# A gated attention block on one core: products of ones before x, weight loads in pieces, closer last merges, more buffers in the tail

## The chip, the cores and the metric

The kernel runs on one core of a Trainium2 chip. A core has TensorE (PE, matrix products into PSUM; its weight loads are shown as PEld), VectorE (DVE), ScalarE (ACT) and GpSimd (POOL) for elementwise work, and SyncE (SP), which here issues every DMA, in order, on one queue. The metric is the device time of one execution in microseconds, given as the median of several runs. The kernel before took 2000.66 us (three runs, 1995.67 to 2001.24).

## The reference

One encoder layer over x of 2048 x 1024 float32. h is the RMS norm of x. One projection of h gives the queries, keys and values of two attention mixers, two gate paths and two merge gates:

```
qa, ka, va, qb, kb, vb, ga, gb, mg = split(h @ w_in)
ya = banded_attention(norm(qa), norm(ka), va, window 128, sink) * silu(ga)      # 8 heads, 2 key heads
yb = sum_g alpha_g * dilated_group(norm(qb_g), norm(kb_g), vb_g) * silu(gb)     # g: dilation 1, 4, 16; 8 heads each
merged = sigmoid(mg_0 + b_0) * (ya @ w_branch_a) + sigmoid(mg_1 + b_1) * (yb @ w_branch_b)
out = x + merged @ w_out
```

alpha is a softmax over the three groups' log-denominators, so the three groups of one pair of heads must be merged before their gate is applied.

## The kernel before

**Precision.** Every product is made of float16 pairs: an operand v is scaled by a power of two and split into a high part (a copy on ACT) and a low part (v minus high, on DVE); three products, high x high, high x low, low x high, are summed in PSUM. So each operand, the weights too, passes ACT and DVE before TensorE can use it. The scale of a weight tile comes from the sum of its squares: a gain on POOL, squares on ACT, a product with a matrix of ones on TensorE that adds over the partitions (`norm_sum`), and a few small steps on DVE (`norm_pow`).

**Order.** The program's order on each engine is written out by hand. A heap of planned times holds small steps; `at(t, f)` adds one, and `until(t)` emits all that are due. While products are emitted, `until` is called between them, so that the steps fall at planned places of TensorE's stream. The planned times only set the order in each engine's queue; on the chip each instruction waits for its operands. `chain` adds steps that must follow one another and try again 0.04 later where a PSUM bank is held.

**Start.** The time is in microseconds. x comes in 16 tiles (`x_load`), each is squared (ACT), scaled (DVE), transposed by TensorE in two halves (`x_turn`) and split into XH and XL. The first two gate chunks (`g_step`) are multiplied in between, from the time when tiles 0 to 3 are there.

**Main part.** The time is in slots. There are 14 units (2 of mixer A, 12 of mixer B: four pairs of heads by three groups) of 8 slots each, so NPAIR = 112. In a slot, TensorE makes the 48 projection products of two 128-row subsets; some slots hold one more product of a gate chunk (FILLS, 24 products). From a subset come norm steps and a DMA transpose of keys and queries (`turn`, tile kq); some 2.9 slots later, an item takes logits, maxima (DVE), exponentials (ACT), the split, a DMA transpose (tile pt) and, LV slots behind its start, the products with the values (`values`, tile pv). Groups 1 and 2 are stored to DRAM (zd) and loaded again (zz) where group 0 merges (`b_merge_q`), whose sums (ya) are turned by TensorE into the one PSUM bank pt, gated and stored to DRAM (`YPart`, tile ytd). The weights of the next unit (`w_load`), of gate chunks (`g_load`) and pieces of w_branch and w_out (`piece_load`, of which only squares are taken) pass one after the other through one raw buffer, wraw. Their loads stand in SP's queue among the transposes.

**Drain.** After slot 112 there are no more projections; slots 112 to 116 and 118 hold 48 fill products each, beside the last items and merges.

**Tail.** Again in microseconds. First five times eight merge-gate products (`gate_pair`, `job(5.2, ...)`), while w_out and the next weights are prepared (`prep`, `b_load`, `b_blocks`). Then 32 branch steps (`branch_pair`, 24 products each): gates come from DRAM (`gate_load`, tiles kp and fg), y in four quarters of eight chunks (`y_part`, tile yg, split into Y), branch weights through `br_load`; sums of them (`a_blocks`) are split into mm and stored to DRAM (mtd). At last 56 products of 12 (`group`) of those blocks (`m_load`, tile M) with w_out's, in a fast scheme with seven products for eight, added to x and stored.

## Time and profile before

| | |
|---|---|
| runs (us) | 1995.67, 2000.66, 2001.24 |
| profiled execution: time, span (us) | 1997.88, 1996.1 |
| granted TensorE clock, mean | 0.998 |
| busy PE, DVE, ACT, POOL (us) | 1941.3, 1308.6, 1032.5, 944.1 |
| products | 17570 |
| DMA | 308.45 MB, mean 155 GB/s |

A line of a profile names engine, source line and operation, the tile written and the tiles read, and counts. The chain of waits is the work that ended last, followed back. A row of a wait names who waited for whom. A stretch's row gives, behind the two ends and the length, each engine's busy time (PE, PEld, DVE, ACT, POOL, each with the number of instructions), the granted share of TensorE's clock, the DMA engines' share and GB/s. SPq is SP's queue of DMA issues.

### The profile page before, as it was taken

The page shows a single profiled execution, that of the slowest core. Times are in us where ns is not written, and L with a number is a line of the kernel's source. Part 1 is how long each engine was busy: PE and PEld are TensorE (multiplying, and loading weights), DVE is VectorE, ACT ScalarE, POOL GpSimd, SP SyncE. Part 2 cuts the span into 40 slices and gives each one's busy share as a digit, 9 for nine tenths or more (in the row PEclk, how much of TensorE's full clock was granted, in tenths as well). Part 3 has the DMA queues.
Part 4 walks back from the last instruction along what each step waited for, and adds up shares of the span by engine and source line. Part 5 has one row for each costly group of instructions (what it writes and reads, how often), then busy time and mean ns, then how long its engine had stood idle before and what let it go on. Part 6 is the DMA issues. An engine that isn't in the chain of part 4 may idle for free. (4 is left out here: it accounts for less than half of the span.)

```text
span 1996.1 us, 47810 instructions
## 1 busy us (share of the span) xinstructions
PE 1941.3 (97%) x17570; PEld 1388.7 (70%) x17570; DVE 1308.6 (66%) x3484; ACT 1032.5 (52%) x2369; POOL 944.1 (47%) x2431
## 2 busy tenths in 40 slices
PE   5999999999999999999999899999999999999999
PEld 3567896678878898888989889897544444444444
DVE  6678877887768876677776887768542323765522
ACT  6467655776555566555666555655433433432200
POOL 3254556454547665556666666656311000222533
PEclk9999999999999999999999999999999999999999
DMA  6249986897749696486866877567523325778763
GB/s 245 79 85 172 177 159 138 145 191 146 178 89 198 117 174 148 99 186 131 173 123 129 160 151 152 100 122 142 153 92 116 132 86 183 207 207 260 253 235 145
DMA packets 584316, 308.45 MB, mean 155 GB/s; under 512 B 457488, under 2 KB 526224, under 8 KB 581776
## 3 DMA queue, kind: packets, MB, share of 16 engines
q1 hardware_dynamic: 584080, 305.39, 65.2%
q8 instruction: 137, 2.24, 0.5%
q14 instruction: 99, 0.81, 0.1%
HBM read 129.91 MB, written 65.27 MB: 98 GB/s over the span
## 5 line engine op out<-in xcount | busy, mean ns | idle before, releaser
L627 PE MATMUL pj<-wl,XH 128*128 128x128 f16 (+2 forms) x2816 | 714.2, 268 | 0.0
L627 PE MATMUL pj<-wh,XL 128*128 128x128 f16 (+2 forms) x2816 | 711.6, 269 | 0.0
L627 PE MATMUL pj<-wh,XH 128*128 128x128 f16 (+2 forms) x2816 | 708.0, 268 | 1.3 <-DVE vt L663 1.3
L627 PEld LDWEIGHTS <-XH 128*128 128x128 f16 x5632 | 577.6, 113 | 64.0 <-issue 1.8
L627 PEld LDWEIGHTS <-XL 128*128 128x128 f16 x2816 | 317.0, 113 | 26.1
L792 DVE CUSTOM_DVE_ANT_0 pr<-s,b,ubuf 128x256 f32<-128x256 f32 (+3 forms) x512 | 218.9, 464 | 57.7 <-PE s L777 55.6
L298 PEld LDWEIGHTS <-wh 128*128 128x128 f16 x1280 | 125.6, 98 | 158.6 <-issue 8.3
L259 POOL TENSOR_TENSOR rs_t<-rs_y 128x8 f32<-128x8 f32 (+2 forms) x345 | 112.2, 325 | 210.4 <-DVE rs_y L250 161.1
L809 DVE SCALAR_TENSOR_TENSOR p<-pr,p 128x512 f16<-128x512 f32 (+2 forms) x256 | 185.2, 723 | 7.8 <-ACT p L805 7.1
L694 POOL TENSOR_TENSOR rw<-rw,g 128x128 f32<-128x128 f32 (+1 forms) x224 | 139.5, 643 | 80.3 <-DVE rw L687 64.0
L687 DVE TENSOR_TENSOR rw<-rw,qr 128x512 f32<-128x512 f32 (+1 forms) x112 | 115.4, 1030 | 90.9 <-POOL vt L656 58.4
L169 POOL TENSOR_TENSOR wraw<-wraw,gn 128x768 f32<-128x768 f32 (+1 forms) x80 | 108.2, 1359 | 122.2 <-DMA wraw<-in_w_mrg_dram 122.2
L805 ACT ACTIVATE p<-pr 128x512 f16<-128x512 f32 (+2 forms) x256 | 159.2, 622 | 10.3 <-DMA pt<-p 4.0
L298 PE MATMUL fps<-Y,wh 128*128 128x512 f16 x512 | 153.8, 381 | 8.6 <-DVE fg L1349 2.0
L645 ACT ACTIVATE rw<-pj 128x256 f32<-128x256 f32 (+1 forms) x224 | 86.5, 386 | 140.4 <-PE pj L627 139.3
L777 PE MATMUL s<-kq 128*128 128x128 f16 (+1 forms) x1856 | 147.1, 218 | 5.6 <-DMA kq<-spl 5.6
L777 PEld LDWEIGHTS <-kq 128*128 128x128 f16 x2016 | 129.9, 98 | 29.0 <-issue 5.7
L709 POOL COPY spl<-spl 128x256 f16<-128x256 f16 (+1 forms) x224 | 92.4, 442 | 121.9 <-DVE spl L704 115.6
L1356 POOL TENSOR_TENSOR kp<-kp,fg 128x512 f32<-128x512 f32 x32 | 43.7, 1366 | 223.8 <-DVE fg L1349 216.6
L1409 PE MATMUL fps<-wt,M 128*128 128x512 f16 x672 | 145.5, 379 | 1.1 <-DVE pr L1423 0.9
L298 PE MATMUL pj<-XH,gh 128*128 128x512 f16 x384 | 145.8, 380 | 0.0
L298 PE MATMUL pj<-XL,gh 128*128 128x512 f16 x384 | 145.7, 380 | 0.0
(190 smaller groups left out, 3632.0 us busy)
## 6 DMA issues: line engine op xcount, KB each, us to landing
wraw<-in_w_units_dram SPq DMA_DIRECT2D x56, 384.0 KB, 4.5
mtd<-mm SPq DMA_DIRECT2D x56, 256.0 KB, 3.0
M<-mtd SPq DMA_DIRECT2D x8, 1792.0 KB, 9.6
mgd<-fg SPq DMA_DIRECT2D x40, 256.0 KB, 2.1
zd<-z SPq DMA_DIRECT2D x128, 66.0 KB, 2.0
zz<-zd SPq DMA_DIRECT2D x64, 132.0 KB, 2.9
xt<-in_x_dram SPq DMA_DIRECT2D x16, 512.0 KB, 10.2
gtd<-yo SPq DMA_DIRECT2D x32, 256.0 KB, 2.8
```

The costliest lines, as they stand in the source:

```text
L169: G.tensor_tensor(v, v, gn[:, c0:c0 + 2].unsqueeze(2).to_broadcast([128, 2, n]), OP.mult)
L259: G.tensor_tensor(tv, yv, yv, OP.mult)
L298: out.append(lambda w=w, xx=xx, ch=ch, i=i: T.matmul(ps[:], lhsT=w[:, ch, c0:c0 + 128], rhs=xx[:, ch, ts], start=(i == 0), stop=(i == n - 1)))
L627: out.append(lambda lhs=lhs, rhs=rhs, ch=ch, a=a, b=b, k=k: T.matmul(ps[:, a:b], lhsT=lhs[:, ch, :], rhs=rhs[:, ch, a:b], start=(k == 0), ...
L687: V.tensor_tensor(q, q, self.rr[:, :n].unsqueeze(2).to_broadcast([128, n, HD]), OP.mult)
L694: G.tensor_tensor(q[:, i, :un.nq, :], q[:, i, :un.nq, :], g, OP.mult)
L709: G.tensor_copy(sp[:, i, nh:, :, :], sp[:, i, nq:nh, ::-1, :])
L777: T.matmul(self.sv[j][:, o:o + k1 - k0], lhsT=q[:, h, :], rhs=kt[:, un.nq + kh + v * un.nk, k0:k1], start=(v == 0), stop=(v == 1))
L792: V.tensor_tensor_reduce(out=self.pv[:, j, self.p0:self.p0 + W], in0=self.sv[j], in1=un.bias[:, self.h0 + j, self.b0:self.b0 + W], scale=I ...
L805: A.activation(self.sp[:, :128 * n], self.pr, AF.Copy, scale=PSC)
L809: V.scalar_tensor_tensor(self.sp[:, 128 * n:], self.pr, PSC, self.sp[:, :128 * n], OP.mult, OP.subtract)
L1409: mm.append(lambda ch=ch, k=k, w=w, i=i: T.matmul(ps[:], lhsT=m[:, a, ch, k, :], rhs=wt[w][:, b, ch, :], start=(i == 0), stop=(i == 11)))
```

## The change

- **Start.** `ones` is filled by VectorE, not GpSimd. A new function `warm` issues products of ones (128x128 by 128x256, as float16) into a bank of pv that nobody reads: 24 before tile 0's transposes, 16 before those of tiles 1, 2 and 3, 12 behind tile 3's.
- **Loads.** A unit's weights are loaded in four issues 0.25 slot apart from 0.1 on (before: two at 0.1, two at 0.6). A gate load becomes two halves, at 5.907 and 6.107. A w_branch or w_out piece becomes four quarters, 0.22 slot apart from 6.3 on (before: one at 5.948); its squares move to 7.15 and 7.5. The gate's sum moves from 7.43 to 7.48.
- **Maximum of y.** Its norm moves from 0.445 and 0.482 to 0.8 and 0.84 slot behind (Y_MAX).
- **Drain.** Steps of items planned past slot 113 run at 0.8 of their distance from it (`drain`), merges past 113 at 0.6 of their spacing (B_LAST).
- **Tail.** Sum, scale and split of the merge-gate weights 1.5 later (T_W). The first three gate loads 1.6 apart. The third quarter of y (q = 2) has six buffers of its own in a new pool yp3, whose loads start with the stage; the second quarter also uses them (5 ahead); the last quarter goes back to three and to steps of 2.8. Four mm buffers in place of three, their stores 1.2 behind the split. In `group`, p1 and u2 take the place of old weight tiles, two buffers each.

```
+B_LAST = 0.6
+DRAIN = 0.8
-G_PREP = (5.907, 6.8, 7.032, 7.43, 7.58, 7.73, 7.88)
-N_PREP = (5.948, 6.756, 7.277)
-Y_MAX = (0.02, 0.445, 0.482)
+G_PREP = (5.907, 6.82, 7.04, 7.48, 7.6, 7.73, 7.88)
+N_PREP = (6.3, 7.15, 7.5)
+B_GAP = (0.25, 0.2, 0.22)
+Y_MAX = (0.02, 0.8, 0.84)
+X_WARM = (24, 16, 16, 16, 12)
-T_Y = (2.0, 0.8, 1.6, 1.5, 3.0, 26.0, 3.0, 1.4)
+T_Y = (2.0, 0.8, 1.6, 1.5, 4.0, 26.0, 3.0, 1.3, 2.8, 1.6)
-T_W = (0.3, 5.5, 1.1, 8.5, 0.9, 12.5, 13.2, 14.7, 0.9, 0.8)
+T_W = (0.3, 5.5, 1.1, 8.5, 0.9, 14.0, 14.7, 16.2, 0.9, 0.8)
-T_A = (0.3, 0.2, 1.5, 0.8)
+T_A = (0.3, 0.2, 1.5, 0.8, 1.2)
...
-    G.memset(ones[:], 1.0)
+    V.memset(ones[:], 1.0)
...
+    def warm(n):
+        ps = pv_p.tile([128, 512], F32, name="pv")
+        v = ones[:].bitcast(F16)
+        for _ in range(n):
+            T.matmul(ps[:, 0:256], lhsT=v[:, 0:128], rhs=v, start=True, stop=True)
...
+    for t, n in enumerate(X_WARM):
+        at(scale_time(t) + X_CH[2] - .05 if t < 4 else scale_time(3) + X_CH[2] + X_CH[5] + .05, warm, n)
...
+    def drain(t):
+        return min(t, NPAIR + 1 + DRAIN * (t - NPAIR - 1))
...
-                at(s + d, f)
-            v = s + LV[un.kind]
+                at(drain(s + d), f)
+            v = drain(s + LV[un.kind])
...
-            at(t + d, f)
+            at(t + d * (B_LAST if t > NPAIR + 1 else 1), f)
...
+    def piece_load(u, k, j):
+        c = slice(512 * j, 512 * j + 512)
+        h, i = divmod(k - 4, 2)
+        nc.sync.dma_start(out=pre[u][1][:, c], in_=w_bra[k, :, c] if k < 4 else w_out[h, :, 4 * i + j, :])
...
-        steps = [(t + W_STEP[i], w_load, u + 1, (2 * i, 2 * i + 1)) for i in range(2)]
+        steps = [(t + W_STEP[0] + B_GAP[0] * i, w_load, u + 1, (i,)) for i in range(4)]
...
-        chain([(t + G_PREP[0], lambda u=u, c=c: g_load(c, pre[u][0]))]
+        for i in range(2):
+            at(t + G_PREP[0] + B_GAP[1] * i, lambda u=u, c=c, i=i: g_load(c, pre[u][0], (i,)))
...
-        at(t + N_PREP[0], piece_load, u, k)
+        for j in range(4):
+            at(t + N_PREP[0] + B_GAP[2] * j, piece_load, u, k, j)
...
-    def y_part(t, q, ahead):
+    def y_part(t, q, ahead, early=None):
         for c in range(8):
-            b = t + (T_Y[7] if q == 2 else T_Y[2]) * c
-            at(max(t - T_Y[3], b - ahead * T_Y[2]) + .001 * c, y_load, c, q)
+            d = T_Y[7] if q == 2 else T_Y[8] if q == 3 else T_Y[2]
+            b = t + d * c
+            at(max(t - (T_Y[3] if early is None else early), b - ahead * d) + .001 * c, y_load, c, q)
...
-    ypool[0] = f2b, 3
+    yp3 = rs2.enter_context(tc.tile_pool(name="yp3", bufs=1, side="right"))
+    ypool[0] = yp3, 6
...
-            mm = f2.tile([128, 4, 2, 128], F16, name="mm", bufs=3)
+            mm = f2.tile([128, 4, 2, 128], F16, name="mm", bufs=4)
...
+            at(now[0] + T_A[4], store, mm, b)
...
-        at(t + .001 * k, gate_load, BCS[steps[k][0]], steps[k][1])
-    y_part(t + T_Y[4], 2, 3)
+        at(t + T_Y[9] * k, gate_load, BCS[steps[k][0]], steps[k][1])
+    y_part(t + T_Y[4], 2, 6, T_Y[4] - .01)
...
-    y_part(t + T_Y[5], 1, 3)
+    y_part(t + T_Y[5], 1, 5)
...
         if k == 13:
+            ypool[0] = f2b, 3
...
-        p1, p5, u2, u3 = (f3.tile([128, 512], F32, name=f"pr{i}", bufs=1) for i in range(4))
+        p1, u2 = (wp.tile([128, 512], F32, name=k) for k in ("wh", "wl"))
+        p5, u3 = (f3.tile([128, 512], F32, name=f"pr{i}", bufs=1) for i in range(2))
```

More of the change, by code (lines that the diff above doesn't have):

```diff
@@ L303, in block_kernel, with g_load @@
     gw = {}
-    def g_load(c, raw=None):
+    def g_load(c, raw=None, parts=(0, 1)):
         if raw is None:
             raw = sp0.tile([128, NCH, 128], F32, name="graw", bufs=2)[:]
-        nc.sync.dma_start(out=raw, in_=w_gate[c])
+        for i in parts:
+            nc.sync.dma_start(out=raw[:, 4 * i:4 * i + 4, :], in_=w_gate[c][:, 4 * i:4 * i + 4, :])
         gw[c] = [raw]
@@ L990, in sums @@
             if q % 2:
-                YPart(4 + j, q // 2, un.y).plan(t + B_MERGE[5])
+                YPart(4 + j, q // 2, un.y).plan(t + B_MERGE[5] * (B_LAST if t > NPAIR + 1 else 1))
         for d, f in zip(B_MERGE, (collect, exponents, exps, factors, products, sums)):
-            at(t + d, f)
+            at(t + d * (B_LAST if t > NPAIR + 1 else 1), f)
     psq = us.tile([128, 16], F32, name="psq")
@@ L1003, in window @@
         pre[u] = v[:, :1024].rearrange("p (a b) -> p a b", b=128), v[:, 1024:]
-    def piece_load(u, k):
-        if k < 4:
-            nc.sync.dma_start(out=pre[u][1], in_=w_bra[k])
-        else:
-            h, i = divmod(k - 4, 2)
-            nc.sync.dma_start(out=pre[u][1].rearrange("p (a b) -> p a b", b=512), in_=w_out[h, :, 4 * i:4 * i + 4, :])
+    def piece_load(u, k, j):
+        c = slice(512 * j, 512 * j + 512)
+        h, i = divmod(k - 4, 2)
+        nc.sync.dma_start(out=pre[u][1][:, c], in_=w_bra[k, :, c] if k < 4 else w_out[h, :, 4 * i + j, :])
     def piece_square(u, k, half):
@@ L1052, in block_kernel @@
         at(t + G_PREP[0] - .01, window, u)
-        chain([(t + G_PREP[0], lambda u=u, c=c: g_load(c, pre[u][0]))]
-              + [(t + G_PREP[1] + .1 * i, g_gain, c, i) for i in range(2)]
+        for i in range(2):
+            at(t + G_PREP[0] + B_GAP[1] * i, lambda u=u, c=c, i=i: g_load(c, pre[u][0], (i,)))
+        chain([(t + G_PREP[1] + .1 * i, g_gain, c, i) for i in range(2)]
               + [(t + d, f, c) for d, f in zip(G_PREP[2:], (g_square, g_sum, g_pow, g_hi, g_lo))])
@@ L1302, in a_blocks, with store @@
         t = f2.tile([128, 512], F32, name="ms", bufs=1)[:]
+        def store(mm, b):
+            nc.sync.dma_start(out=mtd[qp][:, :, b, ch].rearrange("g p k t -> p g (k t)"),
+                              in_=mm[:].rearrange("p g k t -> p g (k t)"))
+            done.add(("m", qp, ch, b))
         def put(b, v):
-            mm = f2.tile([128, 4, 2, 128], F16, name="mm", bufs=3)
+            mm = f2.tile([128, 4, 2, 128], F16, name="mm", bufs=4)
             hi, lo = split(mm[:, :, 0, :], mm[:, :, 1, :], v.rearrange("p (g t) -> p g t", g=4), inv_m)
@@ L1309, in put @@
             lo()
-            nc.sync.dma_start(out=mtd[qp][:, :, b, ch].rearrange("g p k t -> p g (k t)"),
-                              in_=mm[:].rearrange("p g k t -> p g (k t)"))
-            done.add(("m", qp, ch, b))
+            at(now[0] + T_A[4], store, mm, b)
             yield
```

## The prediction

> **What bounds the kernel now.** I read the page first (engines, slices), then busy time by stretches of 50 us, then TensorE's waits, then the queue of DMA issues around each wait.
>
> ```profile
> span 1996.1 us, 47810 instructions
> ...
> PE 1941.3 (97%) x17570; PEld 1388.7 (70%) x17570; DVE 1308.6 (66%) x3484; ACT 1032.5 (52%) x2369; POOL 944.1 (47%) x2431
> ```
>
> TensorE works for 1941.3 of 1996.1 us, so a change that leaves its products alone can only win from the 54.8 us in which it stands and from time at a lower clock. Where the 54.8 us lie:
>
> ```profile
> 0.00:50.00 50.00, 29.47 (x150) 19.73 (x151) 32.56 (x76) 34.81 (x61) 19.36 (x52) 1.00 0.64 245
> ...
> 1100.00:1150.00 50.00, 44.39 (x578) 40.41 (x576) 42.55 (x123) 28.45 (x71) 32.73 (x93) 0.97 0.84 159
> ...
> 1400.00:1450.00 50.00, 47.16 (x322) 24.34 (x320) 29.45 (x98) 21.36 (x49) 17.40 (x26) 1.00 0.55 140
> ...
> 1650.00:1700.00 50.00, 47.10 (x209) 20.58 (x208) 19.00 (x30) 16.86 (x28) 4.19 (x3) 0.97 0.50 166
> ...
> 1750.00:1800.00 50.00, 45.40 (x209) 20.00 (x207) 30.10 (x44) 13.76 (x20) 12.21 (x9) 1.00 0.74 209
> 1800.00:1850.00 50.00, 48.95 (x226) 21.97 (x225) 32.33 (x49) 12.43 (x18) 11.85 (x10) 1.00 0.80 255
> 1850.00:1900.00 50.00, 48.95 (x227) 22.01 (x226) 23.75 (x32) 10.53 (x16) 26.52 (x20) 1.00 0.77 253
> ```
>
> The first number after the stretch's length is TensorE's busy time, the third from the end its granted clock. 20.5 us are lost in the first stretch (x is on its way), 5.6 at 1100, 2.8 at 1400, and 2.9, 4.6, 1.05 and 1.05 in the tail. In two of these stretches the clock is 0.97, that is 0.03 x 50 = 1.5 us lost on top. The waits of the main part and the drain, by name:
>
> ```profile
> PE s L777 <- DMA kq<-spl: 5.6, 1, 5.6
> PE pt L888 <- DVE ya L989: 3.3, 1, 3.3
> PE pt L888 <- DVE wm L190: 3.1, 2, 2.1
> PE pv L826 <- DMA pt<-p: 2.4, 2, 1.4
> PE pt L183 <- ACT gh L321: 2.2, 2, 1.2
> ...
> PE fps L298 <- DVE pw_p L194: 0.8, 1, 0.8
> PE fps L183 <- ACT wl L208: 0.7, 1, 0.7
> ```
>
> Columns: total us, times, longest. Nearly all of TensorE's standing is in a dozen single events, not in a steady shortage; behind each of them TensorE is the bound again at once. So what an event costs, its removal should bring, unless something is late next.
>
> **Products of ones (start).** 84 products of 128x256 enter TensorE's queue: 24 before tile 0's transposes, 16 before those of tiles 1, 2 and 3, 12 behind tile 3's.
>
> ```profile
> 18.37 1.09 PE L457 MATMUL s<-idf,xt 128*128 128x128 f32 x4
> ...
> 28.94 1.09 PE L457 MATMUL s<-idf,xt 128*128 128x128 f32 x4 [2.78 <-DVE xt L451]
> 29.82 0.63 PE L298 MATMUL pj<-XH,gh 128*128 128x512 f16 x1
> 30.24 0.63 PE L298 MATMUL pj<-XL,gh 128*128 128x512 f16 x1
> ...
> 32.20 0.38 PE L298 MATMUL pj<-XH,gh 128*128 128x512 f16 x1
> 32.41 0.38 PE L298 MATMUL pj<-XL,gh 128*128 128x512 f16 x1
> ```
>
> At 29.82 one 512-wide product follows another after 0.42 us, at 32.20 after 0.21: the clock doubles there. From 28.94 on TensorE is not starved any more, so a full clock from there saves half of 32.20 - 28.94 = 3.26 us, 1.6 us. The start at 28.94 itself waits for DVE's scaling of x and stays. Whether the clock is still full there depends on small batches with idle time between them: I take half, **-0.8 us**. Against it: a cold 256-wide product costs 0.21, and (16 + 16 + 12) x 0.21 = 9.2 us are put into the 10.6 us from 18.37 to 28.94 that already hold four transposes groups of 1.1; 9.2 + 4.4 is 3.0 too long. Bounds -1.6 and +3.0. Moving the fill of ones to VectorE lies in its idle first microseconds.
>
> [...]
>
> ```profile
> 1668.00:1698.00 30.00, 27.10 (x117) 11.53 (x115) 12.59 (x18) 9.13 (x15) 4.19 (x3) 0.94 0.75 245
> ...
> 1691.00:1694.50 3.50, 2.85 (x7) 0.97 (x7) 1.35 (x2) 0.40 (x1) 1.27 (x1) 0.51 0.97 393
> ```
>
> TensorE stood for only 2.9 us in 30, in pieces, and was still given half its clock.
>
> **Loads in spaced pieces (main part).** What made the 5.6 us, in the queue's issues and then on TensorE:
>
> ```profile
> 1112.22 0.35 SPq L308 DMA_DIRECT2D wraw<-in_w_gate_dram  x1
> 1112.62 1.77 SPq L1010 DMA_DIRECT2D wraw<-in_w_out_dram  x1
> 1114.50 1.24 SPq L815 DMA_TRANSPOSE pt<-p  x1
> ...
> 1118.38 4.69 SPq L717 DMA_TRANSPOSE kq<-spl  x2
> ```
>
> ```profile
> 1125.16 0.80 PE L777 MATMUL s<-kq 128*128 128x128 f16 x6 [5.61 <-DMA kq<-spl]
> ```
>
> And what such loads and transposes take from issue to landing (count, KB each, median us):
>
> ```profile
> wraw<-in_w_out_dram SPq DMA_DIRECT2D x4, 1024.0 KB, 6.4
> ...
> wraw<-in_w_out_dram SPq DMA_DIRECT2D x16, 256.0 KB, 3.5
> ...
> kq<-spl SPq DMA_TRANSPOSE x224, 2.8
> ```
>
> A gate load (512 KB) and a w_out piece (1 MB) are issued within 0.8 us, and the transposes queued behind them take 4.69 us to issue alone. After the change the gate load is two halves 0.2 slot apart, and the piece comes 0.39 slot behind it as four quarters 0.22 slot apart (a slot without fill is 48 products of 384 columns, 7.7 us by the 0.21 for 512, and the attention's own products, so some 2 us lie between quarters). By the two w_out rows 1024 KB take 6.4 us and 256 KB 3.5, so 256 KB more costs about 1 us: a transpose then meets one quarter (1 us), not 1.5 MB (6). I count 5.6 + 1.5 for the clock, less 1.1 left over: **-6.0**. The two waits of pv (2.4) come behind gate loads of 512 KB: halves leave a third, **-1.6**. The two waits for wm (3.1) come where the maximum of a gated chunk takes the one PSUM bank just ahead of the next chunk's turn; Y_MAX moves it from 0.445 to 0.8, past that turn's gate: **-2.3**, with the rest for the gate's read, now 0.07 slot ahead. The sum of the gate weights moves 0.05 slot (0.5 us) later and its square loses another square ahead of it on ACT: of 2.2, **-0.8**. The pieces themselves: three more issues for each of eight loads, and the squares wait with 0.54 slot (5 us) for a landing of 3.5; ACT has 52% busy to hide a late one, and if it can't, that is an evacuation late by 1 to 2 us. For new waits of this kind I add two at the size of the longest pv wait, 1.4: **+2.0** (bounds 0 and +10.7, all of it lost). Main part: -10.7 + 2.0 = **-8.7**.
>
> **Last merges (drain).** Past slot 113 items run at 0.8 and merges at 0.6 of their spacing. The last values move from 116.73 to 115.98, the last turn from 118.29 to 117.14: from within slot 118's products to behind slot 116's. A drain slot is 48 products of 0.21, some 10 us, so the chain from values to turn now has 1.16 slots = 12 us. What it needs at the least is seen ahead of the wait:
>
> ```profile
> 1447.95 1.07 POOL zz L982
> ...
> 1449.97 0.44 DVE ya L989
> ```
>
> 2.5 us from POOL's products to the end of the sums, and about as much again (an estimate from these rows) for the small DVE and ACT steps before. The 3.3 should go; the last norm moves in front of the last products, which may take the 0.8 with it, though the tanh of the last product ends as late. **-3.7** (bounds -4.1 and 0: the same wait one slot earlier).
>
> **Tail.** Edits: gate weights' sum 1.5 later (the 0.7 wait for wl goes), six early buffers for the quarter q = 2 of y, gate loads spaced, four mm buffers, stores 1.2 behind, the last quarter of y in steps of 2.8.
>
> ```profile
> 1673.33 9.25 SPq L1142 DMA_DIRECT2D yg<-ytd  x6
> ...
> 1686.82 0.42 SPq L1225 DMA_DIRECT2D wraw<-in_w_brn_dram  x1
> ...
> 1761.48 8.14 SPq L1142 DMA_DIRECT2D yg<-ytd  x5
> ```
>
> and from ACT's waits and operations between 1697 and 1800, and the page's DMA issues:
>
> ```profile
> ACT mm L1200 <- DMA mtd<-mm: 26.8, 12, 4.4
> ```
>
> ```profile
> 1737.34 0.72 ACT L1200 ACTIVATE mm<-ms,ubuf 128x512 f16<-128x512 f32 x1 [1.51 <-DMA mtd<-mm]
> ```
>
> ```profile
> mtd<-mm SPq DMA_DIRECT2D x56, 256.0 KB, 3.0
> ```
>
> The first y load is issued 5 us after the stage begins (1668), behind six gate loads, and the next ones wait for buffers; the branch weights, planned 9 us in, go out at 1686.82, 19 us in. With two gate loads ahead the first y goes out about 2 us sooner and four more follow without waiting. The first then lands near 1675; with four gate loads in between and 1 us for each 256 KB the last chunk lands near 1686 and is split by 1687.5, just before its product at 1668 + 93 products of 0.215 = 1688. So the 2.9 + 1.5 us of 1650 to 1700 go, less 0.4: **-4.0**. The last quarter of y, planned for 1747 (14 steps of 24 products behind the begin, the 5 us lost there, 1.5 more), is issued at 1761, because the queue stands behind merge stores that stand behind mm buffers (26.8 us of ACT's waits). Less lateness from the start and a fourth buffer should bring most of it back, and its product is due six steps of 5.2 us behind the plan's begin, 29 us after it: of 4.6, **-4.0**. Of the 2.1 us in 1800 to 1900, **-1.2** (waits for products held up by the same queue), and **-0.7** for wl. Tail **-9.9** (bounds -11.8 and 0). p1 and u2 in two buffers each: the last stage is TensorE without gaps, nothing.
>
> **Sum.** -0.8 - 8.7 - 3.7 - 9.9 = -23.1 us. The profiled execution took 1997.88 (span 1996.1), the median shown is 2000.66, 2.8 more. 1997.88 - 23.1 = 1974.8, and 2.8 on it gives **1978**.
>
> **Rivals.**
> 1. *The tail's wait only moves.* A block's buffer is held for 0.7 (ACT) + about as much on DVE + 1.2 (the new delay) + 3.0 of landing: 5.6 over four buffers is 1.4 a block, against 4.4 over three, 1.5, before, with 1.5 planned; longer landings raise both. The fourth buffer is then nearly eaten up by the delay and the last quarter of y is as late as now. For it: ACT's 26.8 us; against: the early y loads. 1978 + 9.2 = 1987.
> 2. *The main part's waits come back elsewhere*: pieces spread over more slots meet more transposes. 1978 + 8.7 = 1987. Both together: 1996, so that the change in the end does not do what it says.
> 3. *Slower.* The one wait for keys fell in a unit of group 0, where the loads of zz share the queue; there are four such units, and each has up to ten pieces (four of unit weights, two of gates, four of w_branch or w_out). At 1 us for each piece that a key transpose meets, 4 x 10 = 40 us: 1978 + 40 = 2018; it passes the time before from 0.57 us a piece. Against it: TensorE waited for keys once in 224 transposes, whose median landing is 2.8.
>
> **How the numbers follow.** Forecast 0.70 (own range 1970 to 1985), rival 1 0.12, rival 2 0.09, both 0.05, slower 0.04. 0.3% is 6 us, about what a measurement of this kernel can tell from no change: faster means below 1994.7. The first three cases give 0.91, less 0.03 for their upper ends: faster 0.88, same 0.08, slower 0.04. The range reaches from the sum with all bounds kept (-1.6 - 14.8 - 4.1 - 11.8 = -32.3, so 1968) over rivals 1 and 2 to just under both together: 1968 to 1994.
>
> **What would show it.** Clock: 512-wide products 0.21 apart at once behind tile 4's transposes, or 0.42 (then -0.8 is wrong). Main: no wait of s for kq above 2 us, stretch 1100 to 1150 at 49 or more busy and clock 1.00; pv, wm and gh together below 4 us. Drain: no wait of pt for ya. Tail: branch weights issued within 13 us of the stage's begin, both stretches that lost 2.9 and 4.6 at over 49. TensorE's busy time must stay near 1941 plus the 84 products (9 to 18 us). Wrong it would be if single waits of 1 to 2 us came up in many units, or ACT's wait for mm stayed above 20 us.

## The result and the profile after

The changed kernel takes 1988.59 us (median; 1988.28 to 1992.31), the kernel before 2000.46 (1995.67 to 2001.24): a ratio of 0.9949, interval 0.9934 to 0.9963. It is faster, by 11.9 us at the median and by 10.2 by the ratio, where 23 had been forecast. The forecast of 1978 missed by 10.6 us; the direction and the range hold, the size does not: about half of what was forecast came. Two executions among the runs below, of 4287 and 5255 us, took over twice as long as all others of their kernels and are left out.

The page of the profile after, span and engines:

```profile
span 1986.8 us, 47978 instructions
...
PE 1951.3 (98%) x17654; PEld 1393.6 (70%) x17654; DVE 1303.6 (66%) x3485; ACT 1028.5 (52%) x2369; POOL 942.5 (47%) x2430
```

TensorE now stands for 35.5 us in place of 54.8. Of the 19.3 us, 10.0 are only filled, with the 84 products of ones (busy time 1941.3 to 1951.3); the span fell by the other 9.3. The stretches of 50 us, in the columns explained before (TensorE's busy time first after the length, its granted clock third from the end):

```profile
0.00:50.00 50.00, 40.18 (x246) 27.47 (x247) 34.01 (x80) 35.69 (x63) 21.60 (x52) 0.97 0.64 245
500.00:550.00 50.00, 48.23 (x478) 40.16 (x477) 34.46 (x118) 28.33 (x79) 27.60 (x90) 0.97 0.79 171
1100.00:1150.00 50.00, 45.97 (x592) 41.04 (x591) 43.04 (x125) 30.54 (x77) 33.40 (x97) 1.00 0.89 172
1400.00:1450.00 50.00, 48.81 (x326) 25.05 (x324) 31.73 (x105) 20.13 (x46) 16.82 (x26) 1.00 0.58 141
1650.00:1700.00 50.00, 50.00 (x233) 22.61 (x232) 23.59 (x37) 17.91 (x31) 7.46 (x5) 1.00 0.56 191
1750.00:1800.00 50.00, 45.35 (x199) 19.67 (x197) 31.29 (x47) 14.21 (x22) 12.60 (x9) 0.93 0.85 277
1800.00:1850.00 50.00, 50.00 (x233) 22.63 (x232) 33.70 (x49) 14.04 (x21) 16.41 (x12) 1.00 0.73 215
1850.00:1900.00 50.00, 50.00 (x234) 22.57 (x233) 14.42 (x21) 6.90 (x10) 22.33 (x18) 1.00 0.76 268
```

1650 to 1700 and 1800 to 1900 are full now. 1100 to 1150 has its clock back but still loses 4.0 us, and 1750 to 1800 loses as much as before and 0.07 of its clock besides. 500 to 550 has a clock of 0.97 that it did not have before. TensorE's waits behind the start, by name:

```profile
PE pj L645 <- DVE vt L681: 3.9, 6, 2.2
PE fps L302 <- ACT Y L1163: 2.8, 2, 2.2
PE s L795 <- DMA kq<-spl: 2.7, 3, 1.1
PE pv L844 <- DMA pt<-p: 2.7, 2, 1.4
PE pt L187 <- DVE yo L910: 2.2, 2, 1.8
PE fps L302 <- DVE Y L1166: 1.9, 2, 1.6
PE pt L187 <- ACT gh L326: 1.7, 3, 0.7
```

The wait for keys of 5.6 is gone, and so are the one for ya (3.3) and most of those for wm (3.1). In their place stand the norm for yo (2.2), shorter waits for keys (2.7), and two kinds that were there before and have grown: pj for DVE's evacuation vt (3.9) and waits for Y (4.7). In the list of before these rows read:

```profile
PE fps L298 <- DVE Y L1148: 1.9, 3, 1.3
...
PE pj L627 <- DVE vt L663: 1.3, 3, 0.6
...
PE fps L298 <- ACT Y L1145: 0.8, 2, 0.7
```

Comparing the start of the same product in both traces (the n-th product into the same tile) gives the gain by stage: the start 2.3 us (forecast 0.8), the main part a loss of 1.5 (forecast a gain of 8.7), the drain 2.1 (3.7), the tail 6.8 (9.9). The main part is the large miss. It has two pieces. The product in which keys are waited for before stands at 1125; between the start and there the change falls from 2.3 us ahead to 1.5 behind, in waits of 0.4 to 1.8 us (the longest at 515, with 0.50 of the clock from 515.23 to 518.64). There it gains 5.8, and 3.6 of these are lost again by 1145. Inside the tail the last quarter of y is the second large miss: between 1760 and 1800 of before the change loses 2.0 us where 4.0 of gain were forecast.

### The profile page after: what moved, and what is told of

Read it like the earlier page. It is cut to its first block, busy times and chain, and to the rows that moved or that the text cites. A ratio compares the mean times of both kernels' runs of the same rounds, so it can differ in the third digit from the quotient of the medians.

```text
span 1986.8 us, 47978 instructions
## 1 busy us (share of the span) xinstructions
PE 1951.3 (98%) x17654; PEld 1393.6 (70%) x17654; DVE 1303.6 (66%) x3485; ACT 1028.5 (52%) x2369; POOL 942.5 (47%) x2430
## 5 line engine op out<-in xcount | busy, mean ns | idle before, releaser
L302 PE MATMUL pj<-XH,gl 128*128 128x512 f16 x384 | 145.6, 379 | 0.0
```

Of the source, the lines that this page charges most:

```text
L302: out.append(lambda w=w, xx=xx, ch=ch, i=i: T.matmul(ps[:], lhsT=w[:, ch, c0:c0 + 128], rhs=xx[:, ch, ts], start=(i == 0), stop=(i == n - 1)))
```

## Experiments

My theory after the comparison: most of the single waits that the change removes are real, but in the main part TensorE, once it does not stand, runs into the next engine a few microseconds later; and waits of about 2 us cost a piece of clock besides (the 1.8 us near 512 are followed by 3.41 us at 0.50 of the clock). The rival was that each edit is worth its term and that something unconnected eats it. Ratios are those to the kernel before, with their 95% interval; the change itself stands at 0.9949. The kernel before was measured anew beside each set of runs (medians 1997.9 to 2000.5), so ratios compare better than medians. Where the intervals of two kernels overlap, a difference between them is a likely one and not a proven one. A time inside a run ("near 1139") is that of the trace named.

### The step of the last quarter of y

```
-T_Y = (..., 1.3, 2.8, 1.6)
+T_Y = (..., 1.3, 1.6, 1.6)
```

> The changed kernel with the last quarter of y in steps of 1.6 as before, in place of 2.8. Theory of the prediction (stores and mm buffers make the last quarter late, the step has no part in it): TensorE still waits for Y near 1771 to 1778, time within 2 us of the changed kernel's 1988.6. Rival (the wider step itself puts the last chunks 8 us later, behind the next group's splits on ACT and DVE): the waits of 4.7 us there and the 6.8 us at half clock go, and the time falls by 5 to 7 us, to 1982 to 1984.

Measured: 1984.8 (1983.35 to 1985.28), ratio 0.9919 (0.9904 to 0.9934). The steps of 2.8 cost some 4 us; I had counted them as nothing. The waits for Y and the stretches at half the clock there are gone from the trace (the run's mean clock is 0.997, the change's 0.996). One wait of 1.7 us at 1772 remains, for DVE's product into the gate tile fg.

### The maximum of y back

```
-Y_MAX = (0.02, 0.8, 0.84)
+Y_MAX = (0.02, 0.445, 0.482)
```

> The changed kernel with the norm of the chunk maxima at its old place (0.445, 0.482). Theory of the prediction: the two waits of the turn for wm come back (1.0 and 2.2 us near 291 and 512), the time rises by 2 us to about 1990.5. Rival (the new place only swaps them for a wait of the norm product for the gate, and the longer of the two waits costs a window of half clock, 1.7 us): the waits for yo go with it, the clock near 515 stays full, and the time is the same or up to 2 us lower, 1986.5 to 1988.6.

Measured: 1994.13 (1990.87 to 1998.5), ratio 0.9966 (0.9955 to 0.9977). The move is worth 3.4 us by the ratios and 5.5 by the medians, more than my 2.3, but in another place. TensorE's waits in this run:

```profile
PE pt L187 <- DVE ym L924: 3.7, 1, 3.7
...
PE pt L906 <- DVE wm L194: 2.6, 2, 1.6
```

The waits for wm are back at 2.6, and the change's wait of the norm for yo (2.2) is not in this list: in the main part the move only swaps one for the other. What it is worth lies in the drain, where TensorE now stands 3.7 us ahead of the norm's product (1442 to 1445.7), and a stretch at half the clock follows (the run's mean clock is 0.995). No trace with the drain as before has this wait for ym: it comes with the closer merges, if the norm of the maxima stays at its old place. So the move is worth this beside the drain's edit; alone in the kernel before it was not run.

### All loads of the main part back

```
-N_PREP = (6.3, 7.15, 7.5)
+N_PREP = (5.948, 6.756, 7.277)
...
-        for j in range(4):
-            at(t + N_PREP[0] + B_GAP[2] * j, piece_load, u, k, j)
+        at(t + N_PREP[0], piece_load, u, k)
```

and so for the unit weights and the gate loads.

> The changed kernel with unit weights, gate weights and the w_branch and w_out pieces loaded, and their squares and sums placed, as before the change. Theory of the prediction (the loads in pieces are worth 8.4 us less 2.0 of new waits): the time rises by 6.4 us to 1995, and the 5.6 us wait for kq near 1119 is back. Rival (the removed wait was given back by new waits for sums, keys and evacuations between 785 and 1140): the wait for kq is back, but the waits near 1015, 1087, 1127 and 1139 (0.96, 0.86, 0.77, 2.28 us) are gone or smaller, and the time is within 2 us of 1988.6.

Measured: 1989.5 (1987.37 to 1991.22), ratio 0.9947 (0.993 to 0.9963), no different from the change. TensorE's wait for keys:

```profile
PE s L794 <- DMA kq<-spl: 6.5, 3, 5.1
```

The wait of 5.1 is back at 1119, with two stretches at half the clock (the mean is 0.92 from 1105 to 1125 and 0.91 from 1125 to 1145), and yet the time is the same: in this trace pj does not wait for vt near 1139. The other runs bear this out. In the four traces with a long wait for keys (before, this one, the tail alone, the products of ones alone: 4.8 to 5.9 us) TensorE has no wait of above 0.25 us for vt behind it; in the thirteen without it, there is one of 2.2 us each time (1.6 with the maximum of y back).

### The loads alone

The same edits, put alone into the kernel before.

> The kernel before with the edits of the loads in the main part alone (unit weights in four, gate loads in two halves, w_branch and w_out pieces in four quarters, their squares and the gate's sum later). By the record this is worth -6.0 (kq at 1119 with its clock) - 1.6 (pv) - 0.8 (gh) + 2.0 (new waits) = -6.4: 1994 against 2000. By the run that put the old loads back into the changed kernel (1990.95 against 1988.6) it is worth 0 to 2.4: 1997.6 to 2000. If it is the head start of the removed wait that makes the new waits, the wait of kq at 1119 is gone and a wait of pj for DVE of about 2 us stands near 1139 in its place.

Measured: 1997.57 against 1999.44, ratio 0.9988 (0.9975 to 1.0001): a gain of 2.4 us, with an interval that ends at nothing, where 6.4 were forecast. Here the mechanism can be seen without the other edits. TensorE from 1115 to 1143, the rows with a wait:

```profile
1116.62 0.49 PE L779 MATMUL s<-kq 128*128 128x128 f16 x6 [0.47 <-DMA kq<-spl]
...
1124.02 0.38 PE L184 MATMUL pt<-gsq,ones 128*128 128x1 f32 x2 [1.26 <-ACT gh L323]
...
1136.96 0.22 PE L629 MATMUL pj<-wh,XH 128*128 128x128 f16 x1 [2.22 <-DVE vt L665]
```

The keys' wait is 0.47. 7 and 20 us behind it TensorE stands for 1.26 and 2.22. What DVE did ahead of the second's end (its timeline):

```profile
1132.67 0.94 DVE L811 SCALAR_TENSOR_TENSOR p<-pr,p 128x512 f16<-128x512 f32 x1
...
1134.02 1.28 DVE L345 SCALAR_TENSOR_TENSOR gl<-wraw,ubuf,gh 128x1024 f16<-128x1024 f32 x1
1135.21 0.48 DVE L794 CUSTOM_DVE_ANT_0 pr<-s,b,ubuf 128x256 f32<-128x256 f32 x1
...
1136.02 0.69 DVE L706 TENSOR_TENSOR spl<-rw,spl 128x512 f16<-128x512 f32 x1
1136.63 0.28 DVE L665 SCALAR_TENSOR_TENSOR vt<-pj,vt 128x128 f16<-128x128 f32 x1
```

DVE works without a gap from 1132.67 on: a split, a merge's small steps, the low part of the gate weights (1.28), two maxima, another split, and only then the evacuation vt that frees TensorE's bank. Before, the same instructions stood in the same order, 4.5 us later:

```profile
1138.53 1.28 DVE L343 SCALAR_TENSOR_TENSOR gl<-wraw,ubuf,gh 128x1024 f16<-128x1024 f32 x1
...
1141.14 0.28 DVE L663 SCALAR_TENSOR_TENSOR vt<-pj,vt 128x128 f16<-128x128 f32 x1
```

TensorE's product was there at 1142.20, without a wait:

```profile
1142.20 0.22 PE L627 MATMUL pj<-wh,XH 128*128 128x128 f16 x1
```

So before, DVE was done 0.8 us ahead of TensorE, because TensorE had stood 5.6 us for the keys. The wait had given DVE time to catch up. Without it DVE comes 4.5 us sooner and no more, and TensorE stands until then: DVE's backlog sets the end. The 40 us around it, by stretches, before and with the loads alone:

```profile
1105.00:1125.00 20.00, 14.55 (x208) 13.62 (x206) 16.16 (x43) 12.34 (x30) 14.37 (x41) 0.99 0.88 177
1125.00:1145.00 20.00, 19.84 (x259) 18.75 (x259) 17.68 (x61) 12.02 (x31) 11.11 (x34) 0.93 0.73 162
```

```profile
1105.00:1125.00 20.00, 18.12 (x243) 16.52 (x242) 16.39 (x45) 10.93 (x30) 13.74 (x39) 1.00 0.79 179
1125.00:1145.00 20.00, 17.57 (x203) 15.46 (x201) 18.32 (x63) 12.10 (x30) 13.44 (x43) 0.91 0.82 181
```

TensorE works 34.39 us before and 35.69 with the pieces: of the 5.6 us, 1.3 are left, at about the same mean clock (0.96). DVE is busy for 18.32 of the second 20 us. By the same product, the trace of the loads alone is ahead of before by 3.4 us at 1087, by 9.6 at 1127 and by 3.6 at 1145. So 6.2 us came (the wait and its clock) and 6.0 went within 20 us: 1.3 and 2.2 in the two waits and 1.7 in 3.4 us at half the clock behind the second (0.51 from 1137.9 to 1141.4), which is most of it. In the changed kernel no such stretch follows (1.00 from 1120 to 1150), and 3.6 of 5.8 went. What the loads alone are ahead with at the end of the main part, 3.8 us, is mostly lost in the tail, where 2.9 go between 1680 and 1700 in longer waits for y and a second stretch at half the clock (0.54 from 1687 to 1694.5). Which of the load edits takes the wait for keys away was not run one by one.

### Products of ones, alone and taken away

Into the kernel before: the filling of ones by VectorE, `warm` and its loop, nothing else.

> The kernel before with the products of ones (and ones filled by VectorE) alone. Theory of the prediction: -0.8 us, first gate product near 29.8 still, 1999.7. Rival, read off the two traces (the transposes at full clock bring the start itself forward): the first gate product near 28.7, all products behind 33 us earlier by 2.3, time 1998.2.

Measured: 1999.63 against 2000.06, ratio 0.9999 (0.999 to 1.0009): nothing. Out of the changed kernel:

```
-X_WARM = (24, 16, 16, 16, 12)
+X_WARM = ()
```

> The changed kernel without the products of ones (the list of their numbers is empty; all else as changed). By the record the start is worth 0.8 us, so 1988.6 + 0.8 = 1989.4. By the changed trace alone (2.3 us ahead by 32 us) 1990.9. By the run of the products alone in the kernel before (ratio 0.9999, the 2.8 us ahead at 32 us eaten up by 174 us) the start's gain does not survive: 1988.6, with the wait of pv at 168 us below the 1.42 it has now and single waits elsewhere moved.

Measured: 1985.11 (1981.04 to 1986.19), ratio 0.9924 (0.9908 to 0.994). The changed kernel is faster without the products, by 3.5 us at the medians. None of the three expectations had this. The head start is in the trace of the change (timeline of TensorE at the first gate products):

```profile
28.22 0.63 PE L462 MATMUL s<-idf,xt 128*128 128x128 f32 x4 [1.92 <-DVE xt L456]
28.68 0.38 PE L302 MATMUL pj<-XH,gh 128*128 128x512 f16 x1
28.90 0.38 PE L302 MATMUL pj<-XL,gh 128*128 128x512 f16 x1
```

The products are 0.21 apart at once, 1.1 us sooner than before and with the full clock. With the products alone in the kernel before, 2.8 us of head start at 33 us are 0.2 at 180, behind a wait of pv of 2.0 near 170. In the change the lead over the kernel before is gone at 1020. Why? First, products without a head start:

```
-X_WARM = (24, 16, 16, 16, 12)
+X_WARM = (24,)
```

> The changed kernel with the first 24 products of ones alone (those ahead of tile 0), so that the fill of ones, the extra products and their bank of pv stay, but TensorE is idle again between 5 and 11 us and gets no head start at 31 us. If the head start of about 1 us at 31 us is what costs (TensorE then meets transposes and evacuations that have not landed), the time is that without any products: 1985.1, and the waits of 0.9 to 1.5 near 168, 395, 881, 1015 and 1404 are gone or fewer. If the products themselves or their bank cost it, or if it is chance of the runs, 1988.6.

Measured: 1987.99 (1986.43 to 1990.04), ratio 0.9949 (0.9932 to 0.9965). The start in this run, from 9.2 to 33 us, and TensorE's wait near 175:

```profile
9.20:33.00 23.80, 13.87 (x52) 9.74 (x53) 17.50 (x44) 18.98 (x36) 11.94 (x20) 0.50 1.00 389
```

```profile
175.40 0.72 PE L844 MATMUL pv<-vt,pt 128*128 128x65 f16 x18 [1.92 <-DMA pt<-p]
```

TensorE is at half its clock from 9.2 to 33 us (0.50), with no head start, and the wait of 1.92 and the time of the change are there all the same. So it is not the head start. Then the bank: `warm` takes tiles of pv's pool of two, and an odd number of them moves every later tile to the other bank.

```
+X_WARM = (12, 12)
...
-        at(scale_time(t) + X_CH[2] - .05 if t < 4 else ..., warm, n)
+        at(scale_time(0) + X_CH[2] - .05, warm, n)
```

> The changed kernel with the same first 24 products of ones as in the run before (1988.0), but in two tiles of pv, 12 and 12, both ahead of tile 0, in place of one. The pool of pv has two banks, so one tile (or five, as in the change) lets every later pv tile of the kernel take the other bank, two tiles leave them where they were. If the bank is what costs (every profile with an odd number of such tiles has a wait of pv for pt of 1.4 to 2.1 near 168 or 394, five of the six others have none above 1.1), this takes 1985.1 as without products, and no such wait. If the products cost it themselves, 1988.0.

Measured: 1987.98 (1986.08 to 1990.43), ratio 0.9948 (0.9934 to 0.9962). The wait of pv for pt near 173 is there (2.1), so the bank is not it either. One product alone:

> The changed kernel with one product of ones alone, in one tile of pv, ahead of tile 0. It has next to none of the products' work (one in place of 84) and no head start, but moves every later pv tile to the other bank as the change does. If the bank is what costs, 1988 with a wait of pv for pt of 1.4 or more near 168 or 394. If it is the number of the products, 1985.1 and no such wait. If both runs of this pair lie between, the 3.5 us were chance of the runs.

Measured: 1986.7 (1984.68 to 1986.84), ratio 0.9943 (0.993 to 0.9956), with a wait of pv for pt of 0.9: between the two by the median, nearer to the change (0.9949) than to none (0.9924) by the ratio. The expectation called this the sign of chance. Two pairs differ by 3.5 us at the medians (1988.6 against 1985.1, and below 1983.1 against 1979.6), but in each pair the intervals overlap, and in the kernel before the products cost nothing. In the traces, all ten with more than one product of ones have a wait of pv for a transposed p of 1.3 or more near 170 or 395; of the six without products only before has one. So leaving the products out is probably better here; that they themselves cost 3.5 us is not shown, and why waits follow them is not settled.

### The drain back

```
-B_LAST = 0.6
-DRAIN = 0.8
+B_LAST = 1.0
+DRAIN = 1.0
```

> The changed kernel with the drain as before (items and merges past slot 113 at their full spacing; all else as changed). By the record the drain is worth 3.7 us: the 3.3 us wait of pt for ya near 1442 comes back, 1988.6 + 3.7 = 1992.3. By the changed trace the drain brought 2.1 net (the wait of kq at 1404 of 1.1 is new): 1990.7. If the wait also catches a stretch at half the clock (1.7 us each), as with the maximum of y moved back, 1994.

Measured: 1990.53 (1985.39 to 1994.58), ratio 0.9954 (0.9941 to 0.9967). The drain's edit is worth 1 to 2 us at the medians and by the ratios; the intervals overlap widely, so the time alone does not show that it is worth anything. The trace shows that the wait is back where it was:

```profile
PE pt L906 <- DVE ya L1007: 3.5, 1, 3.5
```

That the removal of 3.5 is worth less has a reason in the lists of the two runs: with the drain's edit, keys are waited for at 1404 (1.1 us), without it not. The runs that keep the drain's edit and leave out the last four groups of products of ones do not have this wait either, so in these traces it comes only where both are.

### The tail alone

The edits of the tail, alone in the kernel before (and `ones` filled by VectorE).

> The kernel before with the edits of the tail alone (six early buffers for the third quarter of y, gate loads spaced, the sum of the merge-gate weights later, four mm buffers with later stores, steps of 2.8 for the last quarter, two more product buffers). By the record the tail is worth 9.9: 2000.5 - 9.9 = 1990.6. By the changed trace 6.8: 1993.7. By what the whole change brought (11.9), less what the maximum of y (5) and the drain (2 to 4) are worth, the tail would have only 3 to 5: 1995.5 to 1997.5. Neither stretch 1650 to 1700 nor the loads of the third quarter depend on the main part, so 1650 to 1700 should stand at 49.5 busy or more in any case.

Measured: 1992.23 (1986.22 to 1995.0), ratio 0.9962 (0.9949 to 0.9975): 7.4 us, between the forecast's 9.9 and what the trace of the change gave (6.8). The tail brings most of what the whole change brings.

### The last quarter sooner, and the stores at once

```
-T_Y = (..., 26.0, 3.0, 1.3, 2.8, 1.6)
+T_Y = (..., 26.0, 1.5, 1.3, 1.4, 1.6)
```

> The changed kernel with the last quarter of y in steps of 1.4 in place of 2.8, begun 1.5 us sooner (planned chunk 7 at 1.5 + 9.8 = 11.3 us behind the begin in place of 3 + 19.6 = 22.6). If the lateness of the quarter is the plan's own, the waits at 1771 to 1778 (5.8 us) and their half clock (3.4) go: 1988.6 - 5.8 to 9.2 = 1979.4 to 1982.8, below the 1984.8 of steps of 1.6. If it is ACT's and DVE's queues (the splits stand behind mm splits that wait for their buffers), the quarter is no earlier than with 1.6, the wait of 1.85 at 1770 stays and the time is 1984.8; waits in the merge blocks may then grow.

Measured: 1983.1 (1981.71 to 1984.25), ratio 0.9916 (0.99 to 0.9933), 5.5 us below the change. That is 1.7 below steps of 1.6 (0.9919), which the runs do not tell apart. So the plan's own lateness was most of it. Next, steps of 1.6 with the stores of mm behind the split at once:

```
-T_A = (0.3, 0.2, 1.5, 0.8, 1.2)
+T_A = (0.3, 0.2, 1.5, 0.8, 0.0)
```

> The changed kernel with the last quarter of y in steps of 1.6 (1984.8 measured) and the stores of mm issued at once behind the split in place of 1.2 later. If the delay eats up the fourth buffer (the record's first rival: 5.6 us of holding over four buffers), ACT's waits for mm fall, the last splits of y come up to 1.2 sooner, and the wait of 1.85 us near 1770 goes: 1982.5 to 1983.5. If the buffers are not what makes the quarter late (the splits of y stand in ACT's and DVE's order behind others), the time stays within 1 us of 1984.8. If a store that goes out at once stands ahead of the loads and waits for DVE's split at the head of the queue, 1986 or more.

Measured: 1980.75 (1978.84 to 1983.9), ratio 0.99 (0.988 to 0.9921), 4 us below the same kernel with the delay at the medians; the intervals overlap. By the same product, 2.6 of the 4 us are in the trace from 1760 on, where the delay acts. ACT's waits for mm's buffers between 1697 and 1800, in the change, with steps of 1.6, and with the stores at once:

```profile
ACT mm L1219 <- DMA mtd<-mm: 25.2, 8, 5.4
```

```profile
ACT mm L1219 <- DMA mtd<-mm: 20.6, 5, 5.7
```

```profile
ACT mm L1219 <- DMA mtd<-mm: 6.9, 3, 3.3
```

With the fourth buffer and the delay together, 26.8 us became 25.2, or 20.6 at the same steps of 1.6. Without the delay, which holds each buffer 1.2 longer, 6.9 are left; about half of the difference (7.3 us) returns as ACT's waits for kp. The tail's stretch is full:

```profile
1750.00:1800.00 50.00, 50.00 (x233) 22.68 (x232) 29.15 (x44) 12.88 (x19) 12.14 (x10) 1.00 0.83 266
```

### Together

Without products of ones, with the sooner quarter:

> The changed kernel without the products of ones, and with the last quarter of y in steps of 1.4 begun 1.5 us sooner: the two edits that were each faster than the change (1985.1 and 1983.1 against 1988.6). If they add up, 1988.6 - 3.5 - 5.5 = 1979.6. If the products of ones cost something only through the phase of the clock's windows and of single waits, this sum isn't reached: 1982 to 1983.5, the same as with the products. Both kernels are beaten in either case.

Measured: 1979.63 (1978.5 to 1983.82), ratio 0.9899 (0.9878 to 0.992). At the medians the two gains add up. With the stores at once as well:

> The changed kernel without the products of ones, the last quarter of y in steps of 1.4 begun 1.5 us sooner, and the stores of mm at once behind the split: the three edits that were each faster. If the store's gain (4.0 at steps of 1.6) is the last wait of the quarter (1.85 to 1.92 us) and its clock (up to 1.7), it comes on top of the two others: 1979.6 - 2 to 3.5 = 1976 to 1977.6. If the sooner quarter had taken the same time out already, 1979.6; then the wait of 1.92 at 1767 stands or has only moved.

Measured: 1979.81 (1978.44 to 1981.83), ratio 0.9907 (0.9889 to 0.9925): no better. In the tail one long wait is left. It is not for Y, and the run before has it too (1.8 us):

```profile
PE fps L302 <- DVE kp L1372: 1.5, 1, 1.5
```

The splits of y, packed more tightly, now hold up the evacuation of a branch product on DVE. Three versions beat both kernels by about the same: steps of 1.6 with stores at once, and these two without products of ones; all lie near 1980, about 19 us below before.

## Why the prediction was right and wrong

**Right: the bound, the sign, most of the tail.** The time before lay in single waits, and removing them made it faster. Of the marks set in the prediction these hold: products 0.21 apart at once, no wait for keys above 2 us, clock 1.00 from 1100 to 1150, no wait for ya, TensorE's busy time. These fail: 1100 to 1150 at 49 busy (45.97), pv, wm and gh together below 4 us (2.7 + 0.2 + 1.7 = 4.6; the halves of the gate loads left pv's 2.4 as it was), 1750 to 1800 above 49 (45.35), and ACT's wait for mm. In the tail the early loads hold: the y loads go out at 1667.91, five at once, and the branch weights 13 us behind the stage's begin (1664.5; 1668.1 before).

```profile
1667.91 2.32 SPq L1160 DMA_DIRECT2D yg<-ytd  x5
...
1677.71 0.33 SPq L1244 DMA_DIRECT2D wraw<-in_w_brn_dram  x1
...
1750.84 1.43 SPq L1160 DMA_DIRECT2D yg<-ytd  x3
```

1650 to 1700 came out full, as forecast: by the same product 5.2 us came there, against 4.0. The losses of 1800 to 1900 went too, all 2.1 us of them where 1.2 had been counted.

**Wrong: "I count 5.6 + 1.5 for the clock, less 1.1 left over: -6.0".** The keys' wait went as reasoned, and with it the clock: 6.2 us came in the trace of the loads alone. The step that failed is the next one, "for new waits of this kind I add two at the size of the longest pv wait, 1.4: +2.0 (bounds 0 and +10.7)". I sized new waits as waits for transposes. The new wait was another kind: DVE's evacuation, in a stretch where DVE was 85% busy (42.55 of 50 us), 20 us behind. It took 6.0 of the 6.2 back there, and 3.6 of 5.8 in the changed kernel. Behind it stands the premise at the head of the prediction, "what an event costs, its removal should bring, unless something is late next": the sum does not look for what is late next. The bound of +10.7 held it; the value taken did not. The second rival's price, that the main part is worth nothing, fits the trace of the change; its mechanism (pieces that meet transposes) was not what the trace shows at 1139. That the time came out at 1988.6, beside the 1987 of rivals 1 and 2, does not tell them apart, since both had nearly the same price; by the trace of the change 10.2 us are missing in the main part and 3.1 in the tail. By the loads alone, the loads are worth 2.4 us, with an interval from nothing to 5.

**Wrong in place: wm and Y_MAX, "-2.3, with the rest for the gate's read".** The waits for wm went (3.1 to 0.2), but the norm now waited for yo (2.2). The edit earned its 3.4 to 5.5 us in the drain, where it keeps the closer merges from a wait for ym; that it was of about the forecast's size is luck. The drain's term of -3.7 rested on this edit, and I had priced it without.

**Drain, -3.7.** The wait for ya went, as reasoned. The edit is worth 1 to 2 us, if that; a wait for keys at 1404 took part of it.

**Start, -0.8.** In the trace I was too careful: 2.3 us came, the clock stayed full (1.00 from 13.47 to 515.23). In the time it was nothing (alone) and perhaps a loss of up to 3.5 (in the changed kernel). The step "so a full clock from there saves half" holds for the stretch; that a saving at 32 us lasts to the end is what failed.

**Tail, -4.0 for the last quarter of y.** I wrote that "less lateness from the start and a fourth buffer should bring most of it back". The first loads went out at 1750.84, 10.6 us sooner than before, but TensorE itself was 8.8 us ahead by then: against its products they were 1.8 us sooner. DVE split the last chunk at 1777.7 (before at 1781.7), 4.0 us sooner and so 4.8 late against the products, because the steps were now 2.8 apart: the last of the eight chunks is planned 7 x 1.2 = 8.4 us later than with 1.6. I named the steps in the list of edits and gave them no cost; taken back to 1.6, they brought 4 us. The first rival's arithmetic of buffers (5.6 us over four) was right in kind: ACT's waits for mm stayed at 25.2, above the mark of 20, and the stores at once brought up to 4 us more.

**Clock.** I booked 3.0 us for the two half-clock stretches of before (0.50 from 1124.44 and from 1691.05 on, 3.41 us each), both of which went, and none for new ones. The trace of the change has three new ones behind the start, one from 515.23 and two from 1774.75 on, each 3.41 us at 0.50, by an estimate up to 1.7 us apiece: up to 5.1 us of the miss.

**The sum of the parts.** Tail -7.4 (alone), loads -2.4 (alone), Y_MAX -3.4 to -5.5 and drain -1 to -2 (taken back), start 0 to +3.5: between -17.3 (the larger gains, nothing for the start) and -10.7 (the smaller ones and the start's loss). The measured -11.9 lies inside, but the span is wide; Y_MAX and the drain, each taken back with the other in place, may count some of the same time twice. Kernels near the forecast's 1978 exist (1979.6 to 1980.8): the quarter of y has to come sooner, and either the start's products go or the stores go out at once. That is not the forecast come true, since none of these edits was in its sum.

## What to carry to other kernels

A long wait of the bounding engine can give the other engines time to catch up, as TensorE's 5.6 us did here for DVE. Before its removal is booked as a gain, look at how long each of them works without a gap in the 20 us behind it, and where its queue first makes the bounding engine wait; where there is such a backlog, it sets the price, and not the wait. Every constant in a change's diff needs a term, also those that look like tuning of the same edit: a step size of 2.8 and a delay of 1.2 cost about 4 us each here, and the loads of the main part alone gained 2.4.

## What the runs showed of the hardware

**What a wait cost in clock depended on where it fell.** In the traces of before and of the change the times between two switches of TensorE's clock are whole multiples of 3.41 us. It switches at 1124.44, 1127.85, 1691.05 and 1694.46 in the one, and at 10.06, 13.47, 515.23, 518.64, 1774.75 and 1781.57 in the other; the longest of these times, the 1256.11 us from 518.64 to 1774.75, is 368 times 3.4133. So the run can be cut into stretches of 3.41 us, beginning at any switch. The same wait for ya in the drain, before and with the tail alone, each with its two stretches:

```profile
1450.45 0.44 PE L888 MATMUL pt<-idf,ya 128*128 128x128 f32 x2 [3.29 <-DVE ya L989]
...
1445.28:1448.69 3.41, 1.88 (x10) 0.86 (x8) 2.88 (x9) 0.82 (x2) 1.31 (x2) 1.00 0.50 154
1448.69:1452.11 3.42, 1.66 (x9) 0.94 (x10) 2.39 (x4) 0.00 (x0) 0.90 (x2) 1.00 0.00 0
```

```profile
1447.35 0.65 PE L905 MATMUL pt<-idf,ya 128*128 128x128 f32 x2 [3.29 <-DVE ya L1006]
...
1444.03:1447.44 3.41, 0.12 (x2) 0.10 (x2) 2.65 (x6) 0.00 (x0) 2.20 (x3) 1.00 0.11 32
1447.44:1450.85 3.41, 3.41 (x10) 1.43 (x11) 1.75 (x4) 0.00 (x0) 0.00 (x0) 0.50 0.20 77
```

Before, the wait is shared by two stretches, TensorE is busy for 1.88 and 1.66 us of them, and the clock stays at 1.00. With the tail alone the wait fills one stretch (0.12 us busy), and the next runs at 0.50. A shorter wait was followed by the same, the change's 1.8 us near 512:

```profile
511.82:515.23 3.41, 1.64 (x14) 1.15 (x13) 1.44 (x3) 2.58 (x5) 2.57 (x13) 1.00 1.12 300
515.23:518.64 3.41, 3.41 (x16) 1.96 (x14) 2.56 (x13) 2.27 (x9) 0.56 (x4) 0.50 1.10 256
```

Five stretches at half the clock lie in the traces of before and of the change between 36 us and the last 15 us. One of them, at 1778.16 in the change, follows another. The other four follow stretches in which TensorE was busy for 0.00 (1121.03) and 1.43 us (1687.64) before, and for 1.64 (511.82) and 1.20 us (1771.33) in the change. Behind the next busier ones, 1.66 (1448.69), 1.75 (510.04) and 1.88 us (1445.28) before and 1.81 us (1139.87) in the change, the clock stayed at 1.00. Busy times are modelled, so figures as close as 1.64 and 1.66 do not tell the two groups apart. Half of 3.41 us, 1.7, is what such a stretch costs a TensorE that is never idle in it, an estimate from the clock of 0.50. With the products of ones alone in the kernel before, the wait for ya (3.28 us, up to 1450.61) was followed by two such stretches (0.50 from 1450 to 1453 and from 1453 to 1456.6); why a second one follows is not settled. So the same wait cost 3.3 us, or by this estimate 5.0 or 6.7. With the tail alone it ends 3.1 us sooner than before (1447.35 and 1450.45); none of that run's edits is in the drain, and yet the clock changed there.

**Twenty-four products of ones alone did not keep the clock up.** In the run that kept the first 24 alone the clock was at 0.50 from 9.20 to 33.00 us (the row above). Before, products of 512 go 0.21 apart from 32.20 on, so the 24 won nothing. In the change, behind its first 24:

```profile
6.64:10.06 3.42, 0.01 (x1) 0.04 (x1) 2.54 (x12) 1.38 (x4) 0.00 (x0) 1.00 1.00 380
10.06:13.47 3.41, 3.41 (x16) 2.84 (x17) 1.90 (x4) 1.75 (x4) 2.04 (x2) 0.50 1.02 416
13.47:100.00 86.53, 81.45 (x493) 49.82 (x491) 60.15 (x137) 52.95 (x98) 32.06 (x68) 1.00 0.38 139
```

The column shows 1.00 for the 3.42 us from 6.64 on, in which TensorE was busy for 0.01, and 0.50 for the next 3.41. The products of the second group are 0.21 apart up to 13.28 and 0.11 from 13.48 on, and the clock then stays full to 515.23. The two runs differ in the four groups that follow the first alone, so these are what kept it up. Before, the clock's column shows 1.00 for 0 to 50 us, where the spacing of the products (0.42 from 29.82, 0.21 from 32.20 on) shows half the clock up to about 32: ahead of 32 us the column does not tell the clock in this trace.
